# Hybrid trunk step: gates of the last twelve output chunks in pairs, by seven half products

## The chip, the cores and the metric

The program runs on 1 core of one Trainium2 chip. The metric is the device time of one execution in microseconds; lower is better. A profile of one execution lies beside it; its times are counted from the first profiled instruction.

## What is computed

Two layers with shared structure process 512 latent tokens and 128 context tokens, 640 columns in all. In each layer a modulated RMS norm gives `xn`, one projection feeds four token mixers (a state-space model called SSM below, a Fourier mixer, attention, a short convolution), and the part that matters here merges them:

```python
branches = jnp.stack([y_ssm, y_fft, y_attn.astype(y_ssm.dtype), y_conv], axis=2)
proj = jnp.einsum('blkw,kwd->blkd', branches, lp['w_branch'])
gates = jax.nn.sigmoid(xn @ lp['w_gate'] + lp['b_gate']).reshape(b, l, N_BRANCH, D_MODEL)
out = jnp.sum(gates * proj, axis=2) @ lp['w_out']
```

`D_MODEL` is 1024 and a branch is 512 wide, so `w_gate` is 1024 x 4096 for the 640 tokens. A gated SwiGLU feed-forward network (FFN) follows in each layer.

## The kernel before

Activations lie channels by tokens: 8 tiles of 128 channels x 640 tokens. Each float32 operand is split in a high and a low part (`split`, lines 319 to 321: a cast on ScalarE, a subtraction on VectorE), and a product is three matmuls: high x high, low weight x high, high weight x low. A token range is cut in two halves of 320 columns (`HALF`), one PSUM bank each. All matmuls are issued at line 239, so groups are told apart by their tiles: `main` for the large products, `side` for those of work that runs beside them.

The order on TensorE is written by hand: what is emitted first runs first. The program keeps a planned clock, `now`, to which `mm` (line 234) adds a price for each matmul: 0.136 us for 320 columns. Side work is written as generators that yield a number of microseconds; `tick` (line 263), which is called after each k step of a main product (six matmuls), resumes the generator whose time has come. Thus planned prices alone decide where side matmuls stand. The other engines' instructions are put in order by a scheduler that takes, among those it expects to be ready, the one emitted first; weights are emitted with a priority of 400 instructions ahead (`weights`, line 323).

The stage in question is `mixer_out` (line 1591) with `merges` (line 1382). It runs over 32 output chunks, ordered by branch (Fourier, convolution, attention, SSM), 8 chunks each. In pass n it emits the gate of chunk n + 1 (8 k steps, 48 matmuls of 320 columns, then a Sigmoid on ScalarE into a tile `m_s`), and the branch product of chunk n (4 k steps, 24 matmuls); VectorE multiplies the product by its gate and adds it to `acc` (lines 1431 to 1434). Gates and products alternate over two buffers of two PSUM banks each (`main_ps`). Weights of a gate are one load of 512 KB into `wraw`, one cast to `whi` and one subtraction to `wlo`, with three buffers each. Branch inputs are `yb` tiles.

Three things run beside it. The side generator `ssm_block` (line 1261) computes the SSM for four blocks: loads, a wait of `SSM_LOAD` = 12 planned us, two groups of 8 small matmuls with `s_EF`, a chain on VectorE in seven steps of `SSM_STEP` = 3 planned us each (tiles `s_t`, result `s_X`, last instruction at line 1338), `SSM_LAST` = 6 planned us, and 24 small matmuls with `s_M` and `s_X`. Its tiles lie in the pool of `merges`. `modulations` (line 679) loads 32 tiles of 512 KB at a planned pace of 10.5 us and makes two VectorE reductions of each (line 696). Before the SSM branch `merges` waits until the SSM is through, and `glu` (line 1359) makes four more products out of its result.

At the end each `acc` is split into the operands of the next product, `w_out` (`merged`, line 1440); these go into the buffers `xh` and `xl` of `xn`. The FFN in `tail` (line 1608) already makes most of its input products by a half-size scheme: `sums` (line 546) forms differences of the operand's quarters, `strassen_weights` (line 362) sums of weight parts in tiles `wsum`, and `strassen` (line 398) makes two chunks at once with seven products of 4 k steps, 84 matmuls in place of 96, over four single PSUM banks.

## Time and profile before

| | us |
|---|---|
| median of 3 runs (2626.26 to 2628.92) | 2628.3 |
| the profiled execution | 2626.34 |
| its span, first to last instruction | 2624.6 |
| TensorE busy in it | 2550.9 |
| VectorE busy | 1802.2 |
| ScalarE busy | 1054.2 |

A busy time is the union of an engine's instructions. Ends of matmuls are modelled: neighbouring matmuls overlap in the records, so their pace is read from the starts. The stage `merges` lies between about 428 and 815 us in the first layer and 1726 and 2112 us in the second.

### The profile page before, as it was taken

How to read it: one execution, taken by the hardware profiler on the slowest of the kernel's cores; microseconds unless marked ns; L12 is line 12 of the kernel's file. 1: busy time of each engine (PE TensorE's matmuls, PEld its weight loads, DVE VectorE, ACT ScalarE, POOL GpSimd, SP SyncE). 2: the span in 40 equal slices, each digit the busy share in tenths (PEclk: the TensorE clock that was granted, in tenths of full speed). 3: DMA queues.
4: the chain of work that ended last, by engine and by line, in shares of the span. 5: the costliest groups of instructions: out<-in, count | busy, mean ns of one | idle time of the engine just before them, and what ended most of it. 6: DMA issues, size and time to landing. Idle time of an engine off the chain costs nothing.

```text
span 2624.6 us, 44979 instructions
## 1 busy us (share of the span) xinstructions
PE 2550.9 (97%) x18038; PEld 2437.4 (93%) x18038; DVE 1802.2 (69%) x3581; ACT 1054.2 (40%) x1793; POOL 188.9 (7%) x316
## 2 busy tenths in 40 slices
PE   8999999999999999999999999999999999999999
PEld 5987898999999899999979879989999998999999
DVE  5988764776565687876669887657676547666755
ACT  5334544233223553433453344443332236433433
POOL 0110000111000100000021100011110001000000
PEclk8999999999999999999999999999999998999999
DMA  6442114565344133432235322156643331223222
GB/s 253 136 150 90 59 61 154 177 208 174 127 123 159 49 105 114 128 97 82 83 117 150 128 91 68 51 185 200 198 156 125 121 113 55 83 81 89 79 77 87
DMA packets 121201, 313.85 MB, mean 120 GB/s; under 512 B 35616, under 2 KB 46432, under 8 KB 120608
## 3 DMA queue, kind: packets, MB, share of 16 engines
q1 hardware_dynamic: 101680, 250.52, 30.9%
q0 software_dynamic: 16432, 55.39, 6.2%
q10 hardware_dynamic: 2880, 5.06, 0.5%
q8 instruction: 142, 2.33, 0.4%
q14 instruction: 67, 0.55, 0.1%
HBM read 268.12 MB, written 42.80 MB: 118 GB/s over the span
## 4 chain that ended last, share of the span: by engine, by line
PE 80%; issue 10%; DVE 5%; ACT 3%; DMA 2%; POOL 0%; SPq 0%; ACTq 0%; DVEq 0%; POOLq 0%
PE main L239 71%; PE side L239 8%; PE side L243 1%; DVE wlo L321 1%; DMA s_EF<-d_et 1%; DVE xl L543 1%; DMA s_M<-d_k 0%; ACT xh L541 0%; DVE sm L918 0%; ACT whi L320 0%; DVE tl L321 0%; ACT pq L1024 0%; DMA yb<-d_br 0%; DVE hh L569 0%; POOL d_r L1257 0%
## 5 line engine op out<-in xcount | busy, mean ns | idle before, releaser
L239 PE MATMUL main<-xh,whi 128*128 128x320 f32 x2848 | 739.5, 317 | 8.3 <-ACT xh L541 5.4
L239 PE MATMUL main<-xl,whi 128*128 128x320 f32 x2848 | 724.0, 312 | 6.8 <-DVE xl L321 4.7
L239 PE MATMUL main<-xh,wlo 128*128 128x320 f32 x2848 | 721.5, 311 | 0.0
L320 ACT CAST whi<-wraw 128x1024 fp32r<-128x1024 f32 (+2 forms) x318 | 297.5, 936 | 775.4 <-PE main L239 622.5
L239 PEld LDWEIGHTS main<-xh,whi 128*128 128x128 f32 x2848 | 493.8, 190 | 33.0 <-issue 20.0
L239 PEld LDWEIGHTS main<-xl,whi 128*128 128x128 f32 x2848 | 498.0, 189 | 11.9 <-DVE xl L321 5.9
L239 PEld LDWEIGHTS main<-xh,wlo 128*128 128x128 f32 x2848 | 498.7, 190 | 0.0
L321 DVE TENSOR_TENSOR wlo<-wraw,whi 128x1024 fp32r<-128x1024 f32 (+2 forms) x318 | 345.0, 1085 | 221.4 <-ACT whi L320 218.4
L239 PE MATMUL main<-yb,whi 128*128 128x320 f32 x1152 | 231.7, 312 | 4.4 <-ACT yb L320 4.3
L1454 DVE SCALAR_TENSOR_TENSOR x<-main,ada,x 128x320 f32<-128x320 f32 (+2 forms) x240 | 94.0, 434 | 193.0 <-PE main L239 192.9
L696 DVE SCALAR_TENSOR_TENSOR ada_j<-ada,ada_c 128x1024 bf16<-128x1024 f32 x160 | 194.9, 1218 | 4.5 <-DMA ada<-wada 3.8
L239 PEld LDWEIGHTS main<-yb,whi 128*128 128x128 f32 x1152 | 184.6, 189 | 5.5 <-ACT yb L320 4.9
L239 PE MATMUL main<-hh,whi 128*128 128x320 f32 x704 | 165.1, 310 | 1.0 <-ACT hh L320 1.0
L239 PE MATMUL main<-hl,whi 128*128 128x320 f32 x704 | 164.5, 309 | 0.0
L239 PE MATMUL main<-hh,wlo 128*128 128x320 f32 x704 | 164.3, 309 | 0.0
L239 PE MATMUL main<-th,whi 128*128 128x320 f32 x480 | 149.3, 311 | 0.0
L239 PE MATMUL main<-th,wlo 128*128 128x320 f32 x480 | 149.2, 311 | 0.0
L239 PE MATMUL main<-tl,whi 128*128 128x320 f32 x480 | 149.0, 310 | 0.0
L321 DVE TENSOR_TENSOR wlo<-wsum,whi 128x512 fp32r<-128x512 f32 (+1 forms) x120 | 103.7, 864 | 52.0 <-ACT whi L320 50.7
L320 ACT CAST whi<-wsum 128x512 fp32r<-128x512 f32 (+1 forms) x120 | 91.6, 763 | 114.3 <-PE main L239 109.8
L239 PE MATMUL main<-yb,wlo 128*128 128x320 f32 x576 | 132.2, 311 | 0.0
L239 PEld LDWEIGHTS main<-hh,whi 128*128 128x128 f32 x704 | 118.6, 188 | 4.1 <-issue 2.6
(346 smaller groups left out, 3785.3 us busy)
## 6 DMA issues: line engine op xcount, KB each, us to landing
ada<-wada SPq DMA_DIRECT2D x96, 512.0 KB, 4.1
wraw<-wfi SPq DMA_DIRECT2D x88, 512.0 KB, 3.5
wraw<-wgate SPq DMA_DIRECT2D x64, 512.0 KB, 3.5
wraw<-win SPq DMA_DIRECT2D x50, 512.0 KB, 3.6
wraw<-wfo SPq DMA_DIRECT2D x48, 384.0 KB, 3.2
wraw<-wbr SPq DMA_DIRECT2D x32, 512.0 KB, 3.7
d_f<-t_G POOLq DMA_DIRECT2D x16, 512.0 KB, 4.3
d_et<-t_et POOLq DMA_DIRECT2D x16, 512.0 KB, 4.3
```

The costliest lines, as they stand in the source:

```text
L239: self.nc.tensor.matmul(out, lhsT, rhs, **kw)
L243: self.nc.tensor.transpose(out, in_, ident)
L320: self.nc.scalar.copy(out=hi, in_=src)
L321: self.nc.vector.tensor_sub(out=lo, in0=src, in1=hi.bitcast(F32))
L543: nc.vector.scalar_tensor_tensor(out=xl[:, a:b], in0=t[:, a:b], scalar=B[:, s:s + 1], in1=xh.bitcast(F32)[:, a:b], op0=ALU.add, op1=ALU.su ...
L696: nc.vector.scalar_tensor_tensor(out=junk, in0=w, scalar=1.0, in1=sc[:, s, :], op0=ALU.mult, op1=ALU.mult, accum_out=self.ada[l][:, o + t, ...
L1454: self.anchor = nc.vector.scalar_tensor_tensor(out=x[:, o:o + n], in0=p, scalar=gcol[:, s:s + 1], in1=x[:, o:o + n], op0=ALU.mult, op1=ALU ...
```

## The change

From the point at which the SSM is through, gates are computed in pairs of chunks by the same seven half products that the FFN uses. The VectorE steps of the SSM are planned at 2 us each in place of 3, so it is through earlier. Its tiles move to a pool of their own on the right side of the memory; when the SSM is done, that pool is released and `sums_late` puts the operand's sums and differences there (36 VectorE and 12 ScalarE instructions, and 4 and 4 more in `place`). Three passes later (`GATES_LATER`), at an even chunk, the PSUM pool becomes one of four single banks, `place` overwrites a quarter of `xn` with its difference, and the remaining gates are made two at a time, both ahead of their two branch products. Products and the GLU evict two halves of 320 columns from then on.

```diff
-SSM_LOAD, SSM_STEP, SSM_LAST = 12.0, 3.0, 6.0
+SSM_LOAD, SSM_STEP, SSM_LAST = 12.0, 2.0, 6.0
+GATES_LATER = 3
...
+    def sums_late(self, pool, xs):
+        nc, V = self.nc, self.nc.vector
+        n = KD // 2
+        part = lambda k, h: tuple(x[:, h * HALF:(h + 1) * HALF] for x in xs[k])
+        forms = {"B11": [part(k, 0) for k in range(n)], "B21": [part(n + k, 0) for k in range(n)],
+                 "B22": [part(n + k, 1) for k in range(n)], "T1": [part(k, 1) for k in range(n)],
+                 "T2": [], "T3": [], "T4": []}
+        t1s, pair = [], lambda: [self.t(pool, [128, NT], tag, F32R, bufs=6) for tag in ("th", "tl")]
+
+        for k in range(n):
+            w1, w2 = [self.t(pool, [128, 1024], "wsum", bufs=2) for _ in range(2)]
+            for b, (xh, xl) in ((w1, xs[k]), (w2, xs[n + k])):
+                V.tensor_add(out=b[:, :NT], in0=xh.bitcast(F32), in1=xl.bitcast(F32))
...
+            t1 = t1s[-1][:, o]
+            V.tensor_sub(out=t1, in0=b11, in1=b12)
+            V.scalar_tensor_tensor(out=t2, in0=t1, scalar=-1.0, in1=b22, op0=ALU.mult, op1=ALU.subtract)
+            V.tensor_sub(out=t3, in0=b22, in1=b12)
+            V.tensor_add(out=b21, in0=t2, in1=b21)
+            for name, t, p, c in (("T2", t2, p24, slice(0, HALF)), ("T4", b21, p24, slice(HALF, NT)), ("T3", t3, p3, o)):
+                forms[name].append(tuple(x[:, c] for x in p))
+                self.split(*forms[name][-1], t)
+
+        def place():
+            for k in range(n):
+                self.split(*forms["T1"][k], t1s[k // 2][:, k % 2 * HALF:k % 2 * HALF + HALF])
+        return forms, place
...
+        def gates(k, d):
+            V = nc.vector
+            n = k * KD + d
+            s, u = [self.t(pool, [128, NT], "m_s") for _ in range(2)]
+            s0, s1, u0, u1 = [x[:, o:o + HALF] for x in (s, u) for o in (0, HALF)]
+
+            def use(step, ps):
+                if step in ("P1", "U2", "P5"):
+                    nc.scalar.copy(out={"P1": s0, "U2": s1, "P5": u1}[step], in_=ps)
+                elif step == "P4":
+                    nc.scalar.activation(out=u0, in_=ps, func=AF.Copy, scale=-1.0)
+                elif step == "U3":
+                    two = lambda ap: ap.rearrange("p (a b) -> p a b", a=2)
+                    self.anchor = V.tensor_tensor(out=two(u), in0=ps.unsqueeze(1).to_broadcast([128, 2, HALF]),
+                                                  in1=two(u), op=ALU.add)
+                    nc.scalar.activation(out=u, in_=u, func=AF.Sigmoid, scale=-1.0, bias=bias(n + 1))
+                else:
+                    o = s0 if step == "P2" else s1
+                    V.tensor_add(out=o, in0=ps, in1=o)
+                    nc.scalar.activation(out=o, in_=o, func=AF.Sigmoid, bias=bias(n))
+            self.strassen(self.A["wgate"][l, n], self.A["wgate"][l, n + 1], forms, use)
+            sig.extend((s, u))
...
+            if forms is None and ssm["done"]:
+                self.sp = freed()
+                forms, place = self.sums_late(self.sp, xs)
+                since = n
+            ready = forms is not None and n >= since + GATES_LATER
+            if done == n:
+                if place:
+                    self.main_banks(True)
+                    place()
+                    place = None
+                gates(k, d)
+                done += 2
+            elif done == n + 1 and done < len(order) and not (ready and done % 2 == 0):
+                gate(*order[done])
+                done += 1
...
-            if n < KD:
-                self.anchor = nc.vector.tensor_mul(out=two(acc[d]), in0=pp[:, :, :HALF], in1=two(s))
-            else:
-                self.anchor = nc.vector.tensor_mul(out=two(s), in0=pp[:, :, :HALF], in1=two(s))
+            for b, sv, av in self.pieces(pp, s, acc[d]):
+                self.anchor = nc.vector.tensor_mul(out=av if n < KD else sv, in0=b, in1=sv)
+            if n >= KD:
                 nc.vector.tensor_add(out=acc[d], in0=acc[d], in1=s)
...
+            ps = tc.alloc_tile_pool(name=f"p2s{l}", bufs=2, side="right", reuse_waits="tile")
+            late = []
...
-                    yield from self.ssm_block(p, l, b, ycm[b])
+                    yield from self.ssm_block(ps, l, b, ycm[b])
+
+            def freed():
+                ps.release()
+                late.append(tc.alloc_tile_pool(name=f"p2g{l}", bufs=2, side="right", reuse_waits="tile"))
+                return late[0]
```

## Rows read from the trace of the kernel before

**Rows 1.** The page: busy us, share and count of each engine.

```profile
PE 2550.9 (97%) x18038; PEld 2437.4 (93%) x18038; DVE 1802.2 (69%) x3581; ACT 1054.2 (40%) x1793; POOL 188.9 (7%) x316
```

**Rows 2.** Stretches: us, busy PE, PEld, DVE, ACT, POOL; clock, DMA share, GB/s.

```profile
645.90:815.00 169.10, 169.10 (x1155) 169.06 (x1154) 99.33 (x137) 47.42 (x56) 8.04 (x15) 1.00 0.43 137
1942.40:2111.50 169.10, 169.10 (x1155) 169.06 (x1155) 99.21 (x137) 47.42 (x56) 8.04 (x15) 1.00 0.43 136
```

**Rows 3.** Timeline of PE in one pass: start, us, line, tiles, shape, count.

```profile
649.55 0.46 PE L239 MATMUL main<-xh,whi 128*128 128x320 f32 x2
...
656.59 0.46 PE L239 MATMUL main<-yb,whi 128*128 128x320 f32 x2
...
660.11 0.50 PE L239 MATMUL main<-xh,whi 128*128 128x320 f32 x2
```

**Rows 4.** Timeline of PE in the FFN: first matmuls of two pairs.

```profile
947.00 0.31 PE L239 MATMUL main<-xh,whi 128*128 128x320 f32 x1
...
959.32 0.31 PE L239 MATMUL main<-xh,whi 128*128 128x320 f32 x1
```

**Rows 5.** Stretches as in Rows 2: three FFN pairs; six FFN pairs.

```profile
929.40:966.40 37.00, 37.00 (x255) 37.00 (x254) 32.87 (x49) 19.94 (x35) 0.00 (x0) 1.00 0.35 111
...
1026.00:1100.00 74.00, 74.00 (x507) 74.00 (x506) 64.72 (x102) 40.09 (x71) 0.00 (x0) 1.00 0.42 122
```

**Rows 6.** DVE by shape, FFN then merges: busy us, mean ns | idle before.

```profile
L696 DVE SCALAR_TENSOR_TENSOR ada_j<-ada,ada_c 128x1024 bf16<-128x1024 f32 x8 | 9.7, 1217 | 0.1
L321 DVE TENSOR_TENSOR wlo<-wsum,whi 128x512 fp32r<-128x512 f32 x8 | 5.5, 683 | 0.0
...
L321 DVE TENSOR_TENSOR wlo<-wraw,whi 128x1024 fp32r<-128x1024 f32 x4 | 4.9, 1222 | 4.6 <-ACT whi L320 4.6
L1656 DVE TENSOR_TENSOR f_s<-main,f_s 128x320 f32<-128x320 f32 x9 | 4.4, 485 | 0.0
...
L1434 DVE TENSOR_TENSOR acc<-acc,m_s 128x640 f32<-128x640 f32 x7 | 5.7, 821 | 0.0
```

**Rows 7.** First pair of the FFN: the waits of PE in its timeline.

```profile
921.35 0.38 PE L239 MATMUL main<-xh,whi 128*128 128x320 f32 x1 [1.35 <-DVE f_s L1681]
...
922.66 0.41 PE L239 MATMUL main<-xl,whi 128*128 128x320 f32 x1 [0.78 <-DVE xl L321]
...
925.00 0.63 PE L239 MATMUL main<-xl,whi 128*128 128x320 f32 x1 [1.63 <-DVE xl L321]
```

**Rows 8.** Stretch as in Rows 2: the first pair of the FFN.

```profile
919.70:928.40 8.70, 4.93 (x21) 4.18 (x20) 6.45 (x13) 2.28 (x5) 0.00 (x0) 0.80 0.19 60
```

**Rows 9.** Timeline of PE: `w_out` begins; its eighth k step.

```profile
815.03 0.46 PE L239 MATMUL main<-xh,whi 128*128 128x320 f32 x2
...
821.19 0.46 PE L239 MATMUL main<-xh,whi 128*128 128x320 f32 x2
```

**Rows 10.** Timeline of DVE: a product's multiplication; the last split of the stage.

```profile
649.75 0.82 DVE L1433 TENSOR_TENSOR m_s<-main,m_s 128x640 f32<-128x640 f32 x1 [3.19 <-PE main L239]
...
820.12 0.82 DVE L321 TENSOR_TENSOR xl<-acc,xh 128x640 fp32r<-128x640 f32 x1
```

**Rows 11.** Timeline of DVE: last instruction of the SSM chain, blocks 1, 3, 4.

```profile
480.99 0.28 DVE L1338 TENSOR_TENSOR s_X<-s_t,s_t 64x128 f32<-64x128 f32 x1
...
586.79 0.29 DVE L1338 TENSOR_TENSOR s_X<-s_t,s_t 64x128 f32<-64x128 f32 x1
...
638.88 0.29 DVE L1338 TENSOR_TENSOR s_X<-s_t,s_t 64x128 f32<-64x128 f32 x1
```

**Rows 12.** Timeline of PE: first matmuls that read them, same blocks.

```profile
488.39 0.61 PE L239 MATMUL side<-s_X,s_EF 128*128 128x80 f32 x4
...
589.84 0.61 PE L239 MATMUL side<-s_X,s_EF 128*128 128x80 f32 x4
...
640.85 0.61 PE L239 MATMUL side<-s_X,s_EF 128*128 128x80 f32 x4
```

**Rows 13.** Stretch as in Rows 2: the SSM chain of block 1.

```profile
456.50:488.20 31.70, 31.70 (x218) 31.70 (x218) 29.55 (x40) 10.41 (x19) 3.41 (x8) 1.00 0.52 171
```

More of the change, by code (lines that the diff above doesn't have):

```diff
@@ L417, in strassen @@
             use(step, bank)
+    def sums_late(self, pool, xs):
[10 more added lines that the diff above has]
+                V.tensor_add(out=b[:, :NT], in0=xh.bitcast(F32), in1=xl.bitcast(F32))
+            b11, b12, t3 = [w1[:, i:i + HALF] for i in (0, HALF, NT)]
+            b21, b22, t2 = [w2[:, i:i + HALF] for i in (0, HALF, NT)]
+            o = slice(k % 2 * HALF, k % 2 * HALF + HALF)
+            if k % 2 == 0:
+                t1s.append(self.t(pool, [128, NT], "t1", bufs=2))
+                p3 = pair()
+            p24 = pair()
+            t1 = t1s[-1][:, o]
[10 more added lines that the diff above has]
+        return forms, place
     def gemm(self, ps, w, w0, wstep, m, xs, kts):
@@ L1368, in glu @@
                 s = self.t(pool, [128, 8, 80], "m_s")
-                nc.scalar.activation(out=s.rearrange("p t k -> p (t k)").rearrange("p (a b) -> p a b", a=2),
-                                     in_=ps[:, :, :HALF], func=AF.Sigmoid)
+                for b, sv in self.pieces(ps, s.rearrange("p t k -> p (t k)")):
+                    nc.scalar.activation(out=sv, in_=b, func=AF.Sigmoid)
                 y = self.t(pool, [128, NT], "m_y", bufs=1)
@@ L1379, in glu, with merges @@
         return out
-    def merges(self, pool, l, ycm, acc, xs, ssm):
+    def merges(self, pool, l, ycm, acc, xs, ssm, freed):
         nc = self.nc
-        two = lambda ap: ap.rearrange("p (a b) -> p a b", a=2)
         yb = lambda: self.t(pool, [128, NT], "yb", F32R, bufs=12)
@@ L1389, in merges @@
         sig, w, out = [], None, []
+        forms, place, since = None, None, 0
         def load(k, tiles):
@@ L1400, in load @@
                 ys[k].append((hi, lo))
+        bias = lambda n: self.vec[l][:, V_BGATE + n:V_BGATE + n + 1]
         def gate(k, d):
@@ L1405, in gate @@
             s = self.t(pool, [128, NT], "m_s")
-            nc.scalar.activation(out=two(s), in_=pg[:, :, :HALF], func=AF.Sigmoid,
-                                 bias=self.vec[l][:, V_BGATE + n:V_BGATE + n + 1])
+            for b, sv in self.pieces(pg, s):
+                nc.scalar.activation(out=sv, in_=b, func=AF.Sigmoid, bias=bias(n))
             sig.append(s)
+        def gates(k, d):
[19 more added lines that the diff above has]
+            sig.extend((s, u))
         load(1, range(4))
         gate(*order[0])
+        done = 1
         for n, (k, d) in enumerate(order):
@@ L1414, in merges @@
                 ys[0] = self.glu(pool, l, ycm, ys[0])
-            if n + 1 < len(order):
-                k2, d2 = order[n + 1]
-                if d2 == 0:
-                    if k2 == 0:
-                        self.need(ssm)
-                    load(k2, range(2))
-                gate(k2, d2)
-            else:
+            if n + 1 < len(order) and order[n + 1][1] == 0:
+                if order[n + 1][0] == 0:
+                    self.need(ssm)
+                load(order[n + 1][0], range(2))
+            if forms is None and ssm["done"]:
[13 more added lines that the diff above has]
+                done += 1
+            if n + 1 == len(order):
                 for i in range(KD - 1):
@@ L1611, in tail @@
         last = l == L - 1
-        self.main_banks(True)
+        if not self.single:
+            self.main_banks(True)
         with tc.tile_pool(name=f"p3{l}", bufs=3, reuse_waits="tile") as p:
```

6 lines of the change are left out of this document (3 added, 3 removed).

## The prediction

> **What bounds the kernel now.** The page comes first: TensorE is busy 2550.9 us of a span of 2624.6, VectorE and ScalarE 1802 and 1054 [rows 1]. What counts is the stage. In its second half, from the end of the SSM to the products of `w_out`, TensorE is busy 169.1 of 169.1 us at the full granted clock (1.00, the 2.4 GHz level) in both layers, with VectorE at 99 and ScalarE at 47 us [rows 2]. So here every matmul that goes is time, as long as nothing else becomes late. The timeline shows how regular a pass is: a gate begins at 649.55, the branch product at 656.59, the next gate at 660.11 [rows 3], so 48 matmuls take 7.04 us and 24 take 3.52: 0.1467 us each, 10.56 us a pass.
>
> The FFN shows the scheme that is to come. Two of its pairs begin 12.32 us apart [rows 4], 84 matmuls at the same 0.1467. It does so without a gap (74.0 busy of 74.0) while VectorE is busy 64.7 of 74, and 32.9 of 37 [rows 5].
>
> **How many pairs.** The places follow from the planned clock, by arithmetic. A pass costs 72 x 0.136 = 9.82 planned us, and a side generator resumes only at a tick, every 0.82 us. A step of 3 is thus 4 ticks (3.27), one of 2 is 3 ticks (2.45). With seven steps a block is 5.7 planned us shorter, four blocks 22.9. In the kernel before the last SSM product of block 4 stands behind the gate of chunk 17; adding up the yields gives that place at 191.9 planned us, and 169.0 after, inside the gate of chunk 15. Pass 15 finds the SSM done, pass 18 is ready; it still makes gate 19 (19 is odd), pass 19 makes none, and the pairs are 20-21, 22-23 up to 30-31: **six pairs in each layer**. I replayed the clock of the kernel before too: it puts all eight groups of side products where the trace has them.
>
> **The gain.** A pair needs 84 matmuls in place of 96. 12 pairs x 12 x 0.1467 = **21.1 us** off TensorE's path, where nothing else is in the way [rows 2, 3].
>
> The Trainium skill (TensorE: Matmul & The Clock Gate, "Wait — 56ns, not 53.3ns?") gives a warm stream of matmuls a spacing of its columns at 2.4 GHz plus about 2.5 ns, 135.8 ns for 320 columns by my estimate; the 144 matmuls would then be 19.6 us and the forecast 1.5 us higher. The trace has 146.7 ns, and I take that.
>
> **What VectorE gets in a pair.** By the mean durations [rows 6], for two passes: weights, two subtractions of 1024 (1.22) and three of 512 (0.68), four sums of 512: 7.2 us; branch weights 1.2; evictions of the half products, two of 320 (0.485) and one of 640 (0.82): 1.8; four half multiplications and two additions: 3.6; modulations, about 0.9 tile a pass with two reductions of 1.22 each: 4.1. Sum 17.9 of the 19.36 us that 132 matmuls take, 92%, and less in truth, since neighbours overlap in the records. The FFN lives with a measured 89% [rows 5], so I cost the steady pairs at nothing; that cover is gone if weights come late, and then each pair pays its shortage. ScalarE gains four copies, one more Sigmoid part and 2.9 us of casts in 19.4 us and stays under half busy, as it is in the FFN. DMA bytes do not change, and no queue is passed by a moved load except the SSM's own, which keep their place ahead of the block.
>
> **The start of the pairs.** `sums_late` and `place` are 8 x 0.82 + 32 x 0.485 = 22.1 us of VectorE [rows 6] at pass 15. They must be through by the first pair's third product, 4 passes + 24 + 24 matmuls = 49.3 us later. In that time VectorE also has 4.5 passes of weights, multiplications and additions (3.5 each, 15.6), four splits of branch inputs (3.3), the first sums of weights (3.8) and modulations (2.2 a pass, 9.9): 54.7 in all, 44.8 without the modulations. So it fits if the modulations give way. Behind a sum that waits for its ScalarE copy are queued, on VectorE, the multiplication of product 15 and the subtractions for the next weights; TensorE waits for the former at product 16, 17.6 us after product 14's end, and for the latter at the next gate. The bound above is the FFN's own start, where the same sums had one pass of cover: waits of 1.35, 0.78 and 1.63 us [rows 7], and a granted clock of 0.80 on average over 8.7 us [rows 8], which is 1.7 us less work than at 1.00, some 0.7 of them idle anyway. Cost there 3.8 + 1 = 4.8 us. Below is nothing. With three passes of cover I take **1.5 us** a layer.
>
> **The change of PSUM pools.** Gate and product alternate over two double banks. Pass 19 makes no gate, so product 19 gets the buffer a gate would have had. At the end of the stage a new pool opens after product 31 with no gap: `w_out` begins at 815.03 on the beat [rows 9], so the pool's first banks are not those of products, but those of gates. The first pair therefore should find product 19 in its banks and wait for its multiplication: the pass at hand has its last product matmul 0.15 before 649.55 [rows 3] and the multiplication from 649.75 to 650.57 [rows 10], so about **1.2 us** a layer; nothing if the order is the other way.
>
> **The shorter SSM steps.** Block 1's chain ends at 480.99 + 0.28 and TensorE first reads it at 488.39, 7.1 us later; block 3 has 2.8 and block 4 1.7 us to spare [rows 11, 12]. The interval from the side products to that read shrinks by 5.7 planned us, 6.2 real (x 10.56 / 9.82). But the chain is emitted earlier as well: some 14 us of it are its own, the rest of the 29.55 busy in 31.7 us [rows 13] is what was emitted between, 5 us a pass. Six steps of 0.82 us less until its last instruction take 5 us of such work from ahead of it, half a pass or 2.5 us, and late blocks lose the splits of chunk 15's inputs (up to 3.3) from theirs. So the spare time falls by about 3: to 4, 0 and -1 us or better. I take **0.5 us** a layer; bounds are 0 and the rival below. What queues behind a waiting SSM product is every gate and product.
>
> **GLU and end.** At pass 24 GLU, its splits and the first weights of pair 24 meet on VectorE, covered by 12.3 us of pair before product 24. At the end the last split finished at 820.94 and TensorE read it in the k step that began at 821.19 [rows 10, 9]: 0.25 us to spare. Each layer's planned stage is 9.8 us shorter, so about one modulation tile more (2.4 us) falls behind the end, where it can stand ahead of that split. Bounds -0.3 (the split comes earlier, and nothing is won) and 2.4; I take **0.5 us**.
>
> **Sum.** Costs 2 x (1.5 + 1.2 + 0.5 + 0.5) = 7.4; -21.1 + 7.4 = **-13.7 us**. The profiled execution took 2626.34 (span 2624.6), which becomes 2612.6. The median of the runs shown is 2628.3, 2.0 above it, so the forecast for a median is 2614.6.
>
> **Rivals.**
> 1. Nothing is late: the whole 21.1 us stay, 2607.2. For it: the FFN's steady pairs and three passes of cover. Against: VectorE's 54.7 us of work in 49.3.
> 2. The pairs start as badly as in the FFN, in both layers (4.8 each), with the banks (1.2), a split that is late by a tile (2.4) and 1 us at GLU: 18.8 lost, -2.3, so 2626.0.
> 3. Slower: the SSM chain does not move with its emission, since VectorE was already 93% busy in it [rows 13]. TensorE then waits at blocks 3 and 4 for 6.2 - 2.8 = 3.4 and 6.2 - 1.7 = 4.5 us, at block 2 about 0.5. After stalls of that size the granted clock fell in the FFN [rows 7, 8]: up to 1.7 us more each, as worked out there. 11.8 us a layer, 23.6, with the 6.4 of the other costs: -21.1 + 30.0 = +8.9, 2637.2. It decides once the chain's end moves by less than about 2 of the 6.2 us. Against: only what was emitted ahead of the chain can hold it up. The Trainium skill (TensorE: Matmul & The Clock Gate, "Step-by-step: what each phase is for") states that matmuls stay in program order and only weight loads are pulled ahead, by which a late SSM product would hold all gates behind it; the records here come in the written order, too.
> 4. It does not do what it says: the SSM is through later in the plan than I count, and there are five pairs; 3.5 us less gain, 2618.1.
>
> **How the numbers follow.** Forecast 0.53, rival 1 0.22, rival 2 0.11, rival 3 0.10, rival 4 0.04. The range holds the forecast, rivals 1 and 4 and the better part of rival 2: from 2606.0 (full gain, less a us of scatter) to 2624.5. A measurement of this kernel can tell about 0.2%, 5.3 us, from no change, so faster means below 2623: the forecast, rivals 1 and 4, a little of 2, **0.80**; same 0.10; slower 0.10.
>
> **What would show it.** Right: `th` on TensorE from chunk 20 on, 12 pairs, starts of pairs 19.36 us apart within a branch; the stage ends 7 to 10 us earlier in each layer. TensorE's waits in it name VectorE `xl` or `m_s` around the first pair, with less than 3 us. Wrong: waits of `side` on `s_X` of some us with a clock of 0.5 behind them (rival 3), waits on `wlo` or `whi` in every pair (the steady pairs are not free), or a gate of 48 matmuls beyond chunk 19 (rival 4).

## The result: 41 us slower

The kernel after takes **2669.45 us** (median of 4, 2669.09 to 2669.9), the kernel before 2628.61 beside it: ratio **1.0155** [1.014, 1.0169]. The forecast was 2614.6 and faster. The profiled executions differ by 43.5 us (spans 2668.1 and 2624.6), and this is where they lie. A stage of the branches goes here from the first matmul of the first branch product to the last matmul of the last; the row `w_out` from there to the first matmul that reads the FFN's hidden values (`hh`), so it holds the FFN's norm and its first input products as well; and the next first part begins at the end of the FFN. "Waits" sums the gaps of over 0.15 us between TensorE's records, "at 1.2 GHz" the time in which the granted clock was 0.5; both are before -> after.

| stage | us before | us after | waits | at 1.2 GHz |
|---|---|---|---|---|
| first part, layer 0 | 435.2 | 433.6 | 26.0 -> 27.0 | 27.3 -> 20.5 |
| branches, layer 0 | 379.7 | 392.4 | 3.4 -> 17.0 | 3.4 -> 23.9 |
| `w_out`, layer 0 | 169.1 | 179.8 | 7.4 -> 13.2 | 6.8 -> 17.1 |
| FFN, layer 0 | 348.3 | 348.3 | 2.2 -> 2.2 | 0 -> 0 |
| first part, layer 1 | 400.7 | 407.3 | 19.2 -> 20.6 | 13.7 -> 27.3 |
| branches, layer 1 | 378.3 | 389.1 | 2.7 -> 16.9 | 3.4 -> 17.1 |
| `w_out`, layer 1 | 168.9 | 173.0 | 6.1 -> 9.6 | 13.7 -> 10.2 |
| FFN, layer 1 | 344.4 | 344.6 | 0.5 -> 0.5 | 0 -> 0.9 |

Where the clock is at half, half of TensorE's working time is lost. Longer waits plus half of the added slow time less the forecast gain of 10.56 a layer give +13.3 and +10.5 for the branches (measured +12.7 and +10.8), and +10.95 for `w_out` of layer 0 (+10.7). For `w_out` of layer 1 they give +1.8 where +4.1 was measured; the sum is rough, since it counts slow time that falls into a wait as lost twice. So **the gain is there, and some 60 us stand against it**: 23.3 and 21.4 in the branches' stages (what they lost, and the 10.56), 10.7 and 4.1 in `w_out`. The first part holds no edit and moves with its own slow time, as it does from one execution to the next. In layer 1 a wait comes with the pairs as well (TensorE, before and after):

```profile
1358.39 1.28 PE L239 MATMUL main<-xh,wraw 128*32 128x320 f32 x16 [0.42 <-ACT at L725]
...
1382.54 1.28 PE L240 MATMUL main<-xh,wraw 128*32 128x320 f32 x16 [2.67 <-ACT at L762]
```

It is 2.0 to 2.7 us in all 14 kernels with pairs and 0.4 in the five without. Its cause was not tried.

Three stretches of the kernel after, with the columns of [rows 2]: the branches' stage of layer 0, the worst 16 us of it, and its first pair:

```profile
434.70:827.10 392.40, 375.42 (x2553) 372.02 (x2554) 304.14 (x452) 151.83 (x255) 37.80 (x73) 0.97 0.50 154
649.00:665.00 16.00, 9.38 (x55) 8.45 (x53) 16.00 (x32) 7.26 (x13) 0.00 (x0) 0.85 0.33 109
692.68:712.05 19.37, 19.37 (x134) 19.37 (x133) 15.33 (x24) 8.04 (x13) 0.00 (x0) 1.00 0.44 137
```

The pair is what was forecast: no gap, full clock, the next one 19.37 us later. The loss stands 30 us ahead of it. There TensorE works 9.38 of 16 us and VectorE all of them, where the kernel before, at the same place, had 169.1 busy of 169.1 [rows 2]. Product 16 is the first of the attention branch. TensorE's timeline of the kernel after:

```profile
654.31 0.55 PE L240 MATMUL main<-yb,whi 128*128 128x320 f32 x2 [0.50 <-DVE m_s L1508]
...
661.20 1.43 PE L240 MATMUL main<-yb,whi 128*128 128x320 f32 x4 [4.28 <-DVE yb L322]
...
665.35 0.90 PE L240 MATMUL main<-yb,whi 128*128 128x320 f32 x2 [2.19 <-DVE yb L322]
...
669.25 0.73 PE L240 MATMUL main<-xh,whi 128*128 128x320 f32 x2
669.78 0.73 PE L240 MATMUL main<-xh,wlo 128*128 128x320 f32 x2
...
670.69 0.46 PE L240 MATMUL main<-xh,whi 128*128 128x320 f32 x2
670.98 0.45 PE L240 MATMUL main<-xh,wlo 128*128 128x320 f32 x2
```

It waits twice, for the low halves of tiles 2 and 3 of that branch (`yb`). The gate behind it then runs at half the clock, 0.53 us for two matmuls until 670.3, and 0.29 after that. The slow stretch lasts 10.24 us here, from 660.23 on. VectorE's timeline in the same 8 us:

```profile
657.65 1.55 DVE L434 TENSOR_TENSOR wsum<-xh,xl 128x640 f32<-128x640 f32 x2
659.12 0.48 DVE L443 TENSOR_TENSOR t<-wsum 128x320 f32<-128x320 f32 x1
659.52 0.48 DVE L445 TENSOR_TENSOR wsum<-wsum,wsum 128x320 f32<-128x320 f32 x1
659.92 0.48 DVE L444 SCALAR_TENSOR_TENSOR wsum<-t,wsum 128x320 f32<-128x320 f32 x1
660.33 0.82 DVE L322 TENSOR_TENSOR yb<-yb,yb 128x640 fp32r<-128x640 f32 x1
...
661.47 1.29 DVE L322 TENSOR_TENSOR tl<-wsum,th 128x320 fp32r<-128x320 f32 x3
662.67 0.68 DVE L390 TENSOR_TENSOR wsum<-wraw 128x512 f32<-128x512 f32 x1
...
664.48 0.82 DVE L322 TENSOR_TENSOR yb<-yb,yb 128x640 fp32r<-128x640 f32 x1
```

The tiles had landed at 647.4 and 651.0, and ScalarE's casts began at 649.95 and 656.52. Their low halves stand in VectorE's queue behind the sums of `sums_late` (L434 to L446), the second also behind three sums of the first pair's weights (from L390 on). A tile's buffers come free only when product 15 has read them; from the landing to the matmul that reads them, at 656.9 and 657.7 had nothing waited, these low halves have some 9 and 7 us to be made in. The second loss is at the end of the stage, here in `w_out` of layer 0 (ScalarE, TensorE, VectorE, TensorE):

```profile
830.83 1.91 ACT L721 ACTIVATE ada_c<-ada_c 128x2048 f32<-128x2048 f32 x1 [7.82 <-DMA ada_c<-cond]
...
833.59 1.35 ACT L321 CAST xh<-acc 128x640 fp32r<-128x640 f32 x2
834.36 0.90 PE L240 MATMUL main<-xh,whi 128*128 128x320 f32 x2 [2.79 <-ACT xh L321]
...
846.10 0.17 DVE L735 TENSOR_TENSOR ada<-ada,vec 128x16 f32<-128x16 f32 x1
848.22 1.23 DVE L322 TENSOR_TENSOR wlo<-wraw,whi 128x1024 fp32r<-128x1024 f32 x1 [1.94 <-ACT whi L321]
849.36 2.17 DVE L1530 SCALAR_TENSOR_TENSOR x<-main,ada,x 128x320 f32<-128x320 f32 x6
...
849.96 0.41 PE L240 MATMUL main<-xh,whi 128*128 128x320 f32 x1 [2.90 <-DVE x L1530]
```

ScalarE stood for 7.82 us at the Silu of the next layer's modulations, with the casts of the last branch sums behind it. VectorE's first residual came behind the last modulation tiles (L733, L735), two of which were left over because the stage is shorter in the planned clock, and then behind a weight's low half that waited 1.94 us for its cast. Smaller ones in the stage: an SSM product waits 2.85 us for the DMA of `s_EF`, and the products beside GLU 2.4 us in each layer, where the kernel before has no wait.

### The profile page after: what moved, and what is told of

Same layout as the page of the kernel before. It is cut to its first block, busy times and chain, and to the rows that moved or that the text cites. A ratio compares the mean times of both kernels' runs of the same rounds, so it can differ in the third digit from the quotient of the medians.

```text
span 2668.1 us, 45056 instructions
## 1 busy us (share of the span) xinstructions
PE 2554.3 (96%) x17894; PEld 2431.6 (91%) x17894; DVE 1911.9 (72%) x3805; ACT 1109.8 (42%) x1928; POOL 190.4 (7%) x316
## 4 chain that ended last, share of the span: by engine, by line
PE 78%; DVE 11%; ACT 4%; issue 3%; DMA 3%; SPq 0%; POOL 0%; DVEq 0%; ACTq 0%; POOLq 0%
PE main L240 66%; PE side L240 10%; PE side L244 2%; DVE wlo L322 2%; DMA s_EF<-d_et 1%; ACT whi L321 1%; DVE ada_j L733 1%; DMA ada<-wada 1%; DMA yb<-d_br 1%; DVE xl L580 1%; DVE sm L955 0%; DVE tl L322 0%; ACT xh L578 0%; DVE s_t L1363 0%; ACT pq L1061 0%
## 5 line engine op out<-in xcount | busy, mean ns | idle before, releaser
L240 PE MATMUL main<-xl,whi 128*128 128x320 f32 x2656 | 699.8, 314 | 7.7 <-DVE xl L322 5.5
L240 PE MATMUL main<-xh,wlo 128*128 128x320 f32 x2656 | 696.9, 313 | 0.0
L240 PEld LDWEIGHTS main<-xh,whi 128*128 128x128 f32 x2656 | 469.1, 192 | 45.4 <-issue 21.2
L240 PEld LDWEIGHTS main<-xl,whi 128*128 128x128 f32 x2656 | 473.2, 191 | 13.2 <-DVE xl L322 7.0
L240 PEld LDWEIGHTS main<-xh,wlo 128*128 128x128 f32 x2656 | 473.9, 191 | 0.0
L733 DVE SCALAR_TENSOR_TENSOR ada_j<-ada,ada_c 128x1024 bf16<-128x1024 f32 x160 | 195.1, 1219 | 36.7 <-DMA ada<-wada 35.7
L321 ACT CAST whi<-wsum 128x1024 fp32r<-128x1024 f32 x156 | 119.0, 763 | 185.1 <-PE main L240 180.7
L240 PE MATMUL main<-th,whi 128*128 128x320 f32 x624 | 193.5, 310 | 0.0
L240 PE MATMUL main<-th,wlo 128*128 128x320 f32 x624 | 193.4, 310 | 0.0
L240 PE MATMUL main<-tl,whi 128*128 128x320 f32 x624 | 193.3, 310 | 0.0
L322 DVE TENSOR_TENSOR wlo<-wsum,whi 128x1024 fp32r<-128x1024 f32 x156 | 134.8, 864 | 59.2 <-ACT whi L321 57.9
```

What stands on the lines that cost most here:

```text
L240: self.nc.tensor.matmul(out, lhsT, rhs, **kw)
L321: self.nc.scalar.copy(out=hi, in_=src)
L322: self.nc.vector.tensor_sub(out=lo, in0=src, in1=hi.bitcast(F32))
L733: nc.vector.scalar_tensor_tensor(out=junk, in0=w, scalar=1.0, in1=sc[:, s, :], op0=ALU.mult, op1=ALU.mult, accum_out=self.ada[l][:, o + t, ...
```

## The experiments

All ratios are to executions of the kernel before on the same chip, taken together with the run.

| run | median us | ratio, 95% interval |
|---|---|---|
| e1_sums_end | 2663.64 | 1.013 [1.0107, 1.0152] |
| e2_mod_pace | 2665.04 | 1.0134 [1.0113, 1.0154] |
| e3_step3 | 2648.77 | 1.0078 [1.0059, 1.0097] |
| e4_before_step2 | 2637.89 | 1.004 [1.0022, 1.0058] |
| e5_behind | 2683.85 | 1.0211 [1.0185, 1.0236] |
| e6_sums_gp | 2693.06 | 1.0246 [1.0224, 1.0268] |
| e7_no_pairs | 2652.7 | 1.0088 [1.0067, 1.0109] |
| e8_paced | 2660.39 | 1.0113 [1.0082, 1.0143] |
| e9_paced_step3 | 2648.72 | 1.0083 [1.0053, 1.0112] |
| e10_paced_step3_mod | 2643.48 | 1.0074 [1.0052, 1.0096] |
| e11_pace35 | 2629.65 | 1.0015 [0.9998, 1.0031] |
| e12_pace35_silu | 2623.07 | 0.9971 [0.9958, 0.9985] |
| e13_silu_held | 2625.19 | 0.9996 [0.9983, 1.0008] |
| e14_six | 2641.69 | 1.0054 [1.0041, 1.0066] |
| e15_no_pairs | 2628.71 | 1.001 [0.9996, 1.0023] |
| e16_mod96 | 2623.7 | 0.9992 [0.9978, 1.0007] |
| e17_mod96_no_pairs | 2626.23 | 1.0002 [0.9988, 1.0016] |

### The parts one by one

**The tail: modulations sooner.**

```
-MOD_PACE = (10.5, 12.0)
+MOD_PACE = (9.8, 12.0)
```

> The changed kernel with one number changed: the modulation tiles of the merging stage are planned every 9.8 us in place of 10.5 (12 ticks in place of 13), so the last of 32 is emitted before the stage's end and none after it. Theory 1 (the stage became shorter than the modulations' plan; two tiles are left over, and the residuals of w_out and the last splits stand behind them): the waits of 2.8 and 2.9 us at the start of w_out in layer 1 go, with their clock falls, about 10 us there and 4 in the second layer, 2669.5 - 14 = 2655. Theory 2 (too much VectorE work): a denser pace makes the stalls before that grow, 2670 or more.

`w_out` went back to 169.3 and 169.1 us, 14.4 less over both layers: the tail's loss goes with the leftover modulations. The Silu is still there, but it waits 2.36 us for its load in place of 7.82. The branches' stages grew by 6.5 and 6.2 us, with waits of 22.7 us in each, so a longer stage may have helped the Silu. Little was won: denser work on VectorE goes straight into the stalls of the stage.

**The steps, in the kernel before and out of the kernel after.**

```
-SSM_LOAD, SSM_STEP, SSM_LAST = 12.0, 3.0, 6.0
+SSM_LOAD, SSM_STEP, SSM_LAST = 12.0, 2.0, 6.0
```

This is e4; e3 has the two lines the other way round.

> The kernel before with one number changed: SSM steps of 2 planned us, nothing else. It prices the shorter steps by themselves. If the SSM's chain keeps up (the forecast's view): 2628 to 2630. If the shorter steps bring the waits seen in the changed kernel (2.9 us for the loads of block 3 and about 1 for the chain of block 4, with a clock fall after): 2634 to 2640, in the first layer mainly. If the chain does not move with its emission (rival 3 of the forecast): 2650.

> The changed kernel with the SSM's steps at 3 planned us again: the SSM is done two passes later, sums are emitted at pass 17, when the loads of the attention branch are over, and five pairs are left. Theory 1 (order): the wait of product 16 goes (20 us in two layers) and that for the SSM's loads (6 us in the first layer), two pairs less cost 3.5: about 2645. Theory 2 (amount of VectorE work): the sums meet the same load two passes later, and the time is 2669 + 3.5 less the 6 to 8 us of the SSM's own waits, 2665.

The steps alone cost 0.4% [0.22, 0.58], some 10 us, and forecast was 1.0 for both layers. What waits is not only the chain that the prediction counted (`s_X`, 0.9 us, as forecast): SSM products wait for the DMA of `s_EF`, 5.5 us over three blocks of layer 0. With steps of 3 in the kernel after (e3, near its theory 1) those waits are down to 1.4 us and the kernel has five pairs. Product 16's wait is gone, as the sums now stand at pass 17; 3.4 us at a gate and 4.2 at GLU come in its place.

**Without the pairs.** The sums are worked out and not used; each gate stands alone.

```
-GATES_LATER = 3
+GATES_LATER = 99
```

> The kernel after with the pairs left out: the SSM in steps of 2 us, its pool given back, the sums worked out at pass 15 and not used, and every gate alone in double banks as before. So it has the costs up to the first pair and none of the gain. T1 (the gain of the products is 21 us as forecast, the costs stand beside it): 2669 + 21 = 2690 us less what the pairs cost themselves (bank waits at the products behind them, some 3 us per layer), so 2678 to 2692, and the wait of product 16 is there as in the kernel after. Rival (the pairs' own matmuls bring no such gain, or lose it at once): 2655 to 2672.

Neither held. It is 17 us *faster* than the kernel after by the medians, 11.7 by the profiled executions. The tail has the largest part in that: with the stage at its old length `w_out` takes 168.4 and 167.9 us, 16.5 less. Within the branches' stage it is 5.0 and 5.6 us slower; the other 5.5 lie in the first parts. The wait of product 16 is there without any pair:

```profile
655.40 0.56 PE L240 MATMUL main<-yb,whi 128*128 128x320 f32 x2 [0.51 <-DVE m_s L1508]
...
662.29 1.34 PE L240 MATMUL main<-yb,whi 128*128 128x320 f32 x4 [4.28 <-DVE yb L322]
```

### Order or amount: where the sums stand on VectorE

**At the end of a pass.**

```
             if d == KD - 1 and n + 1 < len(order):
                 load(order[n + 1][0], range(2, 4))
+            if forms is None and ssm["done"]:
+                self.sp = freed()
+                forms, place = self.sums_late(self.sp, xs)
+                since = n
```

The same four lines go from the head of the pass.

> The changed kernel with one block moved: the sums are emitted at the end of pass 15, behind the loads and splits of the attention branch's last two inputs, in place of ahead of them. Same work, same six pairs. Theory 1 (queue order on VectorE: the splits stood behind the sums, product 16 waited 4.3 and 2.2 us for them and the clock fell for 10 us after): those waits go in both layers, about 10 us each, 2669.5 - 20 = 2649. Theory 2 (VectorE simply has too much to do there, and something must be late): the wait moves to the multiplications of products 16 and 17 or to the first pair, and the time stays within 5 us of 2669.

This did not test what it was meant to. The SSM is done by the end of pass 14, so the sums stood ahead of the tiles as before and a seventh pair came instead. Product 16 waited 4.35 and 3.52 us, and the time fell by 5.8 us, where a pair more in each layer is 3.5 by its rows.

**Behind the tiles, enforced.**

```
+            if forms is None and ssm["done"] and n >= 2 * KD - 1:
+                self.sp = freed()
+                with self.tc.issue_after(self.low.ins):
+                    forms, place = self.sums_late(self.sp, xs)
+                since = n
```

`self.low` is the last subtraction of the tiles; the four lines at the head of the pass go here too.

> The kernel after, with the sums issued at the end of pass 15 behind the low halves of the attention branch's tiles 2 and 3 on VectorE; the pairs stay at chunks 20 to 30. An earlier edit put the sums at the end of a pass too, but the SSM had ended a pass sooner by then, so its sums stood before those tiles all the same and the kernel got a seventh pair. Here the order on VectorE itself is turned. T1 (the wait of product 16 is one of order: the tiles' low halves stand behind the sums): product 16 no longer waits in either layer, about 10 us per layer with the half clock that follows, so 2649 us (2644 to 2656). T2 (it is one of amount: VectorE has more to do in these passes than they give it): the wait moves to a weight or to the first pair, and the time stays within 5 us of 2669.

Product 16 waits no more, and the kernel is slower still. Product 18 waits instead (a stretch, TensorE, VectorE):

```profile
656.30:697.30 41.00, 32.66 (x209) 31.86 (x208) 40.92 (x72) 14.71 (x27) 0.00 (x0) 0.92 0.25 80
...
682.97 0.90 PE L240 MATMUL main<-yb,whi 128*128 128x320 f32 x2 [7.63 <-DVE m_s L1504]
...
679.08 1.30 DVE L322 TENSOR_TENSOR tl<-wsum,th 128x320 fp32r<-128x320 f32 x3
...
682.09 0.83 DVE L1504 TENSOR_TENSOR m_s<-main,m_s 128x640 f32<-128x640 f32 x1
```

VectorE works 40.92 of 41.00 us. The multiplication of product 17, which ended about 668.3, stands at 682.09 behind sums, their low halves, two modulations and the first pair's weights, and product 18 needs its bank. Order alone only chooses who is late.

**On GpSimd.** As e5, with the sums and differences on the other engine, behind the tiles' last load there:

```
-                V.tensor_add(out=b[:, :NT], in0=xh.bitcast(F32), in1=xl.bitcast(F32))
+                G(out=b[:, :NT], in0=xh.bitcast(F32), in1=xl.bitcast(F32), op=ALU.add)
...
-            V.tensor_sub(out=t3, in0=b22, in1=b12)
+            G(out=t3, in0=b22, in1=b12, op=ALU.subtract)
```

They are 24 a layer (28 here, where `t2` takes two steps), not the 44 of the expectation.

> As the run with the sums behind the tiles, and their 44 additions and differences of each layer go to GpSimd, which is idle there; VectorE keeps the twelve low halves and four differences less. VectorE is relieved by about 20 us in passes 15 to 19. T2 (amount): 5 to 10 us per layer faster than the run with the sums behind the tiles, since the weights' low halves come in time, and the products of passes 16 to 24 wait for nothing. T1 (order alone): within 4 us of that run. Third possibility: GpSimd takes so long over the sums (over 55 us) that the first pair waits for them; then it is slower than that run by what the first pair waits, in both layers.

Slowest of all, 14.84 us at one product. GpSimd's first sums, VectorE's work beside them, TensorE's wait:

```profile
649.31 3.12 POOL L434 TENSOR_TENSOR wsum<-xh,xl 128x640 f32<-128x640 f32 x2
...
651.31 4.32 DVE L1507 TENSOR_TENSOR acc<-acc,m_s 128x640 f32<-128x640 f32 x1
655.55 1.90 DVE L322 TENSOR_TENSOR wlo<-wraw,whi 128x1024 fp32r<-128x1024 f32 x1
...
696.48 0.79 ACT L1448 ACTIVATE m_s<-main,vec 128x640 f32<-128x640 f32 x1
697.33 0.90 PE L240 MATMUL main<-yb,whi 128*128 128x320 f32 x2 [14.84 <-ACT m_s L1448]
```

The addition that takes 0.82 [rows 6] took 4.32 beside GpSimd's sums, and a subtraction of 1.22 took 1.90. And ScalarE, which casts each sum, waited for GpSimd at each cast with the Sigmoid of a finished gate behind it. So it does not separate the theories: relief on one queue was a block in another. The Trainium skill (SBUF — State Buffer, "SBUF: two separate sides") says that VectorE with two operands in SBUF and GpSimd share a port pair, of which one holds the whole while the other blocks; a slowed VectorE agrees with that, but 4.32 us are more than one of those sums beside it (1.56 us, half of the first row) would hold it up, and this run does not show the port itself.

**In eight parts.** The same sums become a side generator that yields before each half of each of its four steps, every part behind the last product's multiplication; what is left of them when the first pair begins is emitted there.

```
+        def adds():
+            for k in range(n):
+                yield 5.0
                 ...
+                yield 5.0
                 for name, t, p, c in ...
+        return forms, place, self.side(adds(), behind=True)
```

> The kernel after, with the same sums in eight parts, one every 5 us of the order's own clock from pass 15 on, each behind the last product's multiplication; pairs still at chunks 20 to 30. The amount of work on VectorE is the same as in the kernel after, only its 22 us piece is cut. T1 (the harm is the one piece: short deadlines, the tiles' low halves here and the evictions in the run with the sums behind the tiles, stand behind 10 us and more of sums): no wait over 2 us between passes 15 and 19, 8 to 10 us per layer less than after, 2649 to 2654 us. T2 (VectorE has too much to do in these passes however it is cut): the waits come back at the first pair or at the weights, 2664 us or more.

Half of it. Passes 15 to 19 have no wait over 0.7 us, as by T1; but the last part now comes too late, and the first pair waits 5.59 and 1.51 us (the stretch of product 16, then TensorE at the pair, in e8):

```profile
649.00:665.00 16.00, 15.31 (x103) 14.79 (x102) 14.82 (x25) 5.32 (x9) 0.00 (x0) 1.00 0.35 107
...
692.37 0.64 PE L240 MATMUL main<-xh,whi 128*128 128x320 f32 x1 [5.59 <-ACT whi L321]
...
694.52 0.64 PE L240 MATMUL main<-xh,wlo 128*128 128x320 f32 x1 [1.51 <-DVE wlo L322]
```

With the same pairs and the same work on VectorE the ratio is 1.0113 against 1.0155 for the kernel after and 1.0211 for e5, so some 11 and 25 us less. In the profiled execution the branches' stages are not shorter than in the kernel after (392.0 and 394.7 us): the pair's waits stand in the place of product 16's. So **cut in parts, the same amount makes no product late**; that it is done in time as well takes the closer spacing of e11. It is one long piece in a queue of short deadlines that does the harm, with little room left over.

### Putting the costs away one at a time

**Steps of 3 with it (e9), then modulations every 10.0 (e10), then parts every 3.5 us (e11).**

```
-SSM_LOAD, SSM_STEP, SSM_LAST = 12.0, 2.0, 6.0
+SSM_LOAD, SSM_STEP, SSM_LAST = 12.0, 3.0, 6.0
-MOD_PACE = (10.5, 12.0)
+MOD_PACE = (10.0, 12.0)
-                yield 5.0
+                yield 3.5
```

> The same, with the SSM's steps back at 3 us: the SSM ends at pass 17, the pairs are five, from chunk 22 on. The run with steps of 3 and the sums in one piece gave 2648.8, with waits of 3.4 us at a gate and 4.2 us at the GLU and the half clock behind them. T1: both waits go and the waits of the SSM's loads stay away: 2648.8 less some 10 us per layer, 2628 to 2638. T2: 2645 to 2652, within 4 us of that run.

> The same again, with the modulations every 10.0 us in place of 10.5, so that the last of the 32 is issued 16 us sooner and none is left over when the branches' stage ends some 9 us earlier. In the kernel after, a pace of 9.8 took the waits of the w_out stage away (15 us over both layers) and put 13 us into the branches' stage. T1 (with the sums cut there is room for the denser modulations): 8 to 12 us less than the run without it, all of it in w_out, 2618 to 2628. T2 (the room is used up): the branches' stage grows by as much, within 4 us of that run.

> As the run with cut sums, steps of 3 us and modulations every 10.0 us, with the eight parts of the sums every 3.5 us in place of 5, so that the last part stands two products earlier. There the last part stood behind product 21, worked out at 695.42 to 701.2, and the first pair waited 5.59 us for a weight and 1.52 for another, in both layers alike. T1 (these waits are of the last part's place, since the weights' sums use the same two buffers): both waits go, and with the half clock that follows 8 to 11 us per layer: 2643 less some 19, 2619 to 2630. T2 (denser sums bring the waits of products and weights back at passes 18 to 21): within 5 us of 2643.

e9 came in by T2: the wait of one gate went and GLU's fell from 4.2 to 2.4 us, and the late first pair (5.59 and 0.77 us) took their place. e10's median is 5 us lower, between the theories and less than the intervals can tell; the second `w_out` is shorter (168.6 us), the first is not (175.0). In both the last part of the sums stood behind product 21 (VectorE, then TensorE, in e10):

```profile
691.66 0.82 DVE L1512 TENSOR_TENSOR m_s<-main,m_s 128x640 f32<-128x640 f32 x1 [5.46 <-PE main L240]
...
695.42 1.56 DVE L436 TENSOR_TENSOR wsum<-xh,xl 128x640 f32<-128x640 f32 x2
...
704.25 0.63 PE L240 MATMUL main<-xh,whi 128*128 128x320 f32 x1 [5.59 <-ACT whi L321]
...
706.41 0.63 PE L240 MATMUL main<-xh,wlo 128*128 128x320 f32 x1 [1.52 <-DVE wlo L322]
```

VectorE idles 5.46 us with the sums at hand. With 3.5 us between the parts the pair begins without a wait, and the time falls by 14 us (T1).

**The Silu.** Its load and itself move into the side work (e12); then both are also queued behind a cast of the weights of `w_out` (e13: `issue_after` around the two, some 80 and 50 planned us ahead of the first modulation there).

```
-        nc.scalar.dma_start(out=sc, in_=self.A["cond2"]...)
-        nc.scalar.activation(out=sc, in_=sc, func=AF.Silu)
...
-            yield start
+            yield start - 10.0
+            nc.scalar.dma_start(out=sc, in_=self.A["cond2"]...)
+            yield 10.0
+            nc.scalar.activation(out=sc, in_=sc, func=AF.Silu)
```

> The same again, with the load and the Silu of the modulations' operand moved from the start of their side work to just ahead of its first use. In the w_out stage of layer 0 ScalarE's queue stood at this Silu, which waited for its DMA, ahead of the casts that the second w_out chunk needs: waits of 2.34 and 1.93 us in the run with modulations every 10.0 us, 175.0 us for the stage against 169.1 before. If the casts stand behind the Silu, the stage comes to 168 to 170 us and the time falls by 4 to 7 us against the run without this edit; if they are late for another reason, nothing changes (within 3 us). With both edits 2613 to 2625, so faster than the kernel before at 2628 if the pairs' gain of 17.6 us (five pairs, two layers) is left over at all.

> The kernel of the two runs before it (sums in eight parts every 3.5 us, steps of 3 us, modulations every 10.0 us), with the load of the modulations' operand issued in the w_out stage behind the last cast of its weights that the order has by then, and its Silu 30 us of the order's clock behind that. In the run that only moved the Silu's place in the program it stood in ScalarE's queue where it had stood before (the ACT row of 811.42 after 7.59 us idle for its DMA, then the casts of xh at 814.17), and the wait of 2.55 us stayed in w_out. T1 (the casts wait for the Silu): that wait goes and w_out of layer 0 comes to 168 to 171 us against 173.6; the whole 2616 to 2625, from 2623. T2 (the casts are late by themselves): it stays at 173 us or more.

e12 is the only one of the seventeen whose interval lies below the kernel before, **0.9971** [0.9958, 0.9985], and not for the reason given. The scheduler put the Silu where it had been (ScalarE, then TensorE, in e12):

```profile
811.42 1.91 ACT L729 ACTIVATE ada_c<-ada_c 128x2048 f32<-128x2048 f32 x1 [7.59 <-DMA ada_c<-cond]
...
814.17 1.35 ACT L321 CAST xh<-acc 128x640 fp32r<-128x640 f32 x2
...
814.94 0.56 PE L240 MATMUL main<-xh,whi 128*128 128x320 f32 x2 [2.55 <-ACT xh L321]
```

What fell were the branches' stages: 374.2 and 375.5 us against 384.4 and 381.9 in e11, whose profiled execution is the longest of its eleven (2638.93); the medians are 6.6 apart. In e11 an SSM product waits 1.95 and 1.43 us for `s_EF` and one beside GLU 3.24 and 3.37, each with 6.83 us or more at 1.2 GHz beside or behind it; in e12 no wait of the first kind is over 0.85, GLU's are 1.64 and 0.74 in layer 0 and 1.60 and 0.73 in layer 1, and none has slow time with it. Over all executions, span times mean granted clock is 2585.7 us in e11 and 2583.7 in e12, and the clock takes 42.3 and 36.0: most of the lead is the clock. The edit moves the same two instructions in those stages too; whether that is the reason was not tried, and e13, which moves them as well, does not keep the lead. In e13 the Silu is out of the way, and the casts no longer wait; the low half does (VectorE, then TensorE, in e13):

```profile
811.09 1.23 DVE L740 SCALAR_TENSOR_TENSOR ada_j<-ada,ada_c 128x1024 bf16<-128x1024 f32 x1 [3.63 <-DMA ada<-wada]
...
812.25 0.82 DVE L322 TENSOR_TENSOR xl<-acc,xh 128x640 fp32r<-128x640 f32 x1
...
813.12 0.56 PE L240 MATMUL main<-xl,whi 128*128 128x320 f32 x2 [2.72 <-DVE xl L322]
```

Two things stood at that spot: the Silu, and a leftover modulation that waits for its own DMA with the last branch sum's low half behind it. `w_out` stayed at 172.7 us.

**The modulations every 9.6 us, on top of e13 (e16).**

```
-MOD_PACE = (10.0, 12.0)
+MOD_PACE = (9.6, 12.0)
```

> The run with the Silu held back, with the modulations every 9.6 us in place of 10.0, so that the last pair of them stands ahead of the last two products on VectorE. In that run the wait of the first w_out chunk moved from the casts to a low half: VectorE's queue idled 3.63 us at a modulation, for the modulation's own DMA, with the low half of the last branch sum behind it, and TensorE waited 2.72 us. T1 (that wait is the modulation's place): w_out of layer 0 comes to 168 to 170 us from 172.7, and 2 to 6 us go, so 2619 to 2623 of its 2625. T2 (denser modulations push back, as in the kernel after at 9.8): the branches' stage grows by 3 us or more per layer, 2627 or more.

`w_out` of layer 0 takes 170.3 us and the waits at its start are gone, as by T1; the branches' stages are 2.3 and 1.6 us longer and the median falls by 1.5, less than the interval can tell.

**Six pairs, on top of e13 (e14).**

```
-GATES_LATER = 3
+GATES_LATER = 2
-                yield 3.5
+                yield 3.0
```

> As the run with the Silu held back, with the first pair at chunk 20 in place of 22 (six pairs) and the eight parts of the sums every 3.0 us, so that they come to stand in 24 us from pass 17 on. T1 (there is room for them in two passes and a half): 3.5 us less than that run (2 pairs x 12 x 0.147), within its noise. T2 (the room of three passes was needed): the first pair or a product waits again, with the half clock behind it, 8 to 12 us per layer: 10 to 25 us more than that run.

T2: the first pair waits 6.49 us for its weights and a product beside GLU 3.28 (6.50 and 3.07 in layer 1); 16.5 us slower than e13.

### What a pair is worth

e13 and e16 once more with `GATES_LATER = 99`, so without their pairs, with the sums (not used) and all else in place.

> As the run with the Silu held back, without the pairs: the sums are worked out and not used, every gate stands alone. Where nothing is late, the difference is the gain of ten pairs of chunks over both layers by itself. T1 (12 matmuls of 0.1467 us less per pair, and nothing else): 10 x 1.76 = 17.6 us slower than that run, less 2 x 2 us for the GLU's waits, so 13 to 18 us, 2635 to 2642. T2 (the pairs' gain is eaten by what they cost where they stand): within 6 us of that run.

> The same without the pairs (sums worked out and not used). With nothing of the pairs' late in w_out, the difference of the two is the ten pairs alone: 17.6 us less the waits that they bring (5.7 us in the branches' stage in the run pair before), so 10 to 14 us slower than the run with them, 2630 to 2636. Rival, that the pairs lose elsewhere what they gain, as the medians of the run pair before say (3.5 us): within 5 us.

Both came in by the second theory. With nothing late, all that was added beside the pairs costs nothing that can be measured: e15 and e17 are at 1.001 and 1.0002. But the ten pairs bring 3.5 and 2.5 us in the medians and not 17.6, within the intervals of the ratios.

With the clock taken out the two comparisons agree. Span times mean granted clock, averaged over the 11 or 12 executions of each, is 2584.3 with pairs and 2590.2 without (e13, e15), and 2585.2 and 2590.4 (e16, e17): 5.9 and 5.2 us less. Most of what is missing from 17.6 went into waits. In the profiled executions e16's branches' stages are 374.5 and 375.7 us against 381.2 and 377.6 in e17, 8.6 less; its waits there are 6.8 longer (13.0 against 6.2), 4.8 of them at the products around GLU, in each layer as here (TensorE, in e16), where e17 has none:

```profile
713.16 0.41 PE L240 MATMUL main<-yb,whi 128*128 128x320 f32 x1 [1.13 <-DVE m_s L1516]
...
716.56 0.85 PE L240 MATMUL main<-yb,whi 128*128 128x320 f32 x4 [0.94 <-DVE yb L322]
...
718.03 0.85 PE L240 MATMUL main<-yb,whi 128*128 128x320 f32 x4 [0.33 <-DVE yb L322]
```

The wait in the first part of layer 1 (2.67 us in e16, 0.42 in e17) takes 2.25 more. The rest of the span, which is what the clock takes, is 38.6 and 37.3 us in e13 and e15, 36.3 and 34.1 in e16 and e17. Why the clock takes more with pairs is open.

## Why the prediction was wrong

- **The gain** was right in its terms: six pairs a layer at chunks 20 to 30, 72 matmuls a layer fewer at 0.1467 us, pairs 19.37 us apart without a gap, and VectorE busy 15.3 of them in the first, below the 17.9 that were added up. The replay of the planned clock held as well, so rival 4 fell.
- **"The start of the pairs"** is the step that failed. It added up 54.7 us of VectorE's work in 49.3 and concluded that it fits if the modulations give way. They did not: an L733 stands between the sums at 639.61 and 646.76. And it asked by when the sums must be done, not who is late while they are made. It named the multiplication of product 15 and the weights as queued behind them; it counted the four splits of branch inputs in the sum, but not that two of them have 7 to 9 us to be made in. In place of 1.5 us a layer: nothing at the pair, 6.97 us of waits at product 16 and a slow clock behind them, some 10 us a layer. In e5 and e8 that wait is gone and others come; where the same sums stand in time and in parts (e15, e17) none is left that can be measured.
- **The clock** was in the sum only for the first pair, and within the FFN's price. Over its four executions the kernel after has span times mean granted clock at 2609.0 and loses 58.7 us to the clock; the kernel before, over the 23 executions beside e16, 2590.4 and 34.2. So of the 43 us between the mean spans some 24 are the clock, which had no line of its own; the other 19 are 39.5 us of added waits less the gain of 21.1.
- **"The shorter SSM steps"**: 0.5 us a layer was forecast, about 5 measured (e4). The chain through VectorE moved as worked out (0.94 us of wait on `s_X`, the end of -1); the load of `s_EF`, for which no deadline was worked out, was late by up to 2.85 us. Rival 3 had the right side and the wrong cause.
- **"GLU and end"**: 0.5 us was taken, with 2.4 as the bound. GLU costs 2.4 of waits, and `w_out` lost 10.7 and 4.1 us. One tile left over was foreseen; two came, with the residual behind them, the Silu ahead of the last casts, and the clock behind those.
- **"The change of PSUM pools"** costs nothing: products 18 and 19 run from 685.64 to the pair at 692.68 without a gap.
- **The steady pairs** at nothing: right, but for the products beside GLU. The 2.25 us in the first part of layer 1 had no term.

What stays open is why the clock takes less in e12 than in e11 and a little more with pairs than without, and where the wait in the first part of layer 1 comes from.

## What to carry to other kernels

Before work is added to an engine's queue, list what else will stand in that queue in the meantime, each with its own deadline, and not only the deadline of the added work: 22 us in one piece made low halves late that had 7 to 9 us, and cut into eight parts that came in time the same work cost nothing that could be measured. Price a stall of TensorE at more than its length: here 39.5 us of added waits came with some 24 us of added loss to the clock. When a stage becomes shorter, ask which paced side work now ends behind it: here that took 15 us of the gain.

## What the runs showed of the chip that was not expected

- A short stall draws a slow stretch behind it: waits of 4.28 and 2.19 us at product 16 had 10.24 us at 1.2 GHz with and behind them, one of 2.85 us for `s_EF` had 6.83. Not each one does: GLU's 1.18, 0.93 and 0.33 us and the 0.94 for `s_X` had none.
- Sums on GpSimd slow VectorE beside them: 4.32 us for an addition of 0.82.
- The time at 1.2 GHz of a stage that holds no edit differs between profiled executions (first part of layer 1: 10.2 to 30.7 us), and its length with it (some 399 to 409 us, of which the pairs' wait is 2.25). Differences under 5 us had to be read from stages, not from spans.
